# Seven-product weight chunks: where the sum of the two lower blocks is read from, and when

## The chip, the cores and the metric

The kernel runs on one core of one Trainium2 chip. The metric is device time in microseconds (us) of one execution. The kernel before took a median of 1622.32 us in 3 runs (1621.99 to 1623.5).

## The reference

One inference step of a two-layer decoder for a prompt of 512 tokens and a group of 8 single-token samples, which share all weights; the kernel treats them as 520 columns. Each layer is half a SwiGLU, a mixer, and half a SwiGLU; the first mixer pools over windows, the second is windowed attention. All data are float32. Cut to what matters here:

```
D_MODEL, D_FF, SEQ, DEC_BATCH = 1024, 2816, 512, 8

def _swiglu(x, wg, wu, wd):
    return (jax.nn.silu(x @ wg) * (x @ wu)) @ wd

for l in range(2):
    x = x + 0.5 * _swiglu(rms(x), gate[l, 0], up[l, 0], down[l, 0])
    x = x + mixer_l(rms(x))
    x = x + 0.5 * _swiglu(rms(x), gate[l, 1], up[l, 1], down[l, 1])
```

There are thus four SwiGLU blocks (called FFN 0 to 3 below), and their three weight matrices are nearly all of the bytes and of the products.

## The kernel before

**Products.** Every float32 operand is split into a high and a low part of type fp32r (`wh`, `wl` for weights; `xh`, `xl`, `th`, `tl`, `hh`, `hl`, `ph`, `pl` for activations), and a product is three matmuls: high by high, high by low, low by high. A matmul has a 128x128 weight tile and 260 columns (half of the 520). One call of `product` (line 612) takes one split weight piece of 128x512 and issues 12 matmuls.

**Seven instead of eight.** Most FFN work uses a seven-product scheme for 2x2 blocks of weights A and activations B. A hidden tile takes the gate block (upper row, A11 and A12, the two halves of the 1024 inputs) and the up block (lower row, A21 and A22); a tile of the down projection takes two blocks of 128 outputs as the two rows. The seven weight pieces are A11, A12, A22 and four sums, up to signs that lie in the activations: S1 = A21 + A22, S2 = A11 + S1, S4 = A12 + S2, S3 = A21 + A11. The 22 blocks of the hidden dimension are done in three parts of 8, 8 and 6: in each part first the hidden tiles, then (in the first two parts) four down chunks in seven products each; the third part's down projection is plain. The first 4, 3, 2 and 3 hidden tiles of FFN 0 to 3 are plain as well. That gives 76 hidden chunks and 32 down chunks in seven products, 108 in all.

**The weight pipeline** is the class `Weights` (lines 140 to 312). A *chunk* is 1 MB of weights in a tile of pool `rawp` (3 buffers of tag `raw`), loaded by DMAs that SyncE issues (`ld`, line 384): two of 512 KB for a gate/up chunk, four of 256 KB for a down chunk. A *piece* is one of the 128x512 views of a chunk; `_split` turns it into `wh` (ScalarE, line 278) and `wl` (VectorE, line 279), five pieces ahead of the product that uses it. `load(i)` issues the DMAs of chunks up to i, `add_up(i)` the sums that DMAs make. `_split` of a piece of chunk i calls `add_up` for chunk i + 1 and `load` for chunk i + 2. In `woven` (down chunks) the pieces of two neighbouring chunks interleave, and in both orders the piece A22 of a chunk is put off until A11 and S1 of the next one are out.

**The sums.** `combos` (line 194) makes them:

- S1 gets a tile `S` of its own, of 256 KB, from pool `splp` (tag `S`, 4 buffers). SyncE loads A21 into it from device memory a second time (`again`), and a DMA that GpSimd issues adds A22 to it from the chunk's `raw` tile (line 205, an accumulating DMA from SBUF to SBUF).
- S3 is made in place by another accumulating DMA on GpSimd's queue: A21 += A11 inside `raw` (line 206).
- S2 and S4 are VectorE additions in place, of A11 (line 212) and A12 (line 218). S2 reads the tile `S` and is its last reader.

Two more tiles of tag `S` hold `ph`, `pl`, activation sums of a part's first pair of hidden tiles (`HiddenSums.more`, line 655), from the second hidden tile of the part to the last product of its down projection; while they live, two `S` buffers are left for the weight chunks. The pooling mixer also borrows tiles of that tag (`pr`, `hrow`).

**Order.** The program is recorded in the order of the code; a scheduler then orders each engine's instructions, and it places each where its own estimate of time lets it. Instructions that pass through `later` keep their recorded order among each other, as do all DMAs of `ld` on SyncE's queue. Each engine's queue and SyncE's DMA queue run strictly in order: an instruction that waits holds all behind it. A tile that is taken from a pool waits for the last reader of the buffer's previous holder.

Of the kernel before, what the change touches and what calls it, by code (L numbers as in the profile page):

```python
# [11 lines left out]
F32 = mybir.dt.float32  # L12
# [3 lines left out]
ALU = mybir.AluOpType  # L16
AX = mybir.AxisListType

P = 128
# [12 lines left out]
NPL = (4, 3, 2, 3)  # L32
# [107 lines left out]
class Weights:  # L140
# [4 lines left out]
    def __init__(self, nc, rawp, splp, chunks_ahead, ahead):  # L145
        self.nc, self.rawp, self.splp = nc, rawp, splp
        self.ca, self.ahead = chunks_ahead, ahead
        self.chunks, self.items = [], []
        self.nl = self.na = self.ns = self.ng = 0
        self.late = None  # L150
        self.slow = set()
        self.part = {}
        self.stop = 10**9
        self.pin = lambda ins: ins

    def chunk(self, *dmas):
        self.chunks.append([list(dmas), None, None])
        return len(self.chunks) - 1

    def piece(self, ch, view):  # L160
# [11 lines left out]

    def load(self, i):
        while self.nl <= min(i, len(self.chunks) - 1):
            self.begin(len(self.chunks[self.nl][0]))
            self.nl += 1

    def begin(self, n):

# [14 lines left out]
    def combos(self, ch, again):  # L194

        G, V, tmp = self.nc.gpsimd, self.nc.vector, {}

        def blk(raw, r, c):
            return rows(raw)[:, r - 1, 4 * c - 4 : 4 * c, :]

        def loaded(raw):
            s1 = self.splp.tile([P, 4, P], F32, tag="S", name="S", bufs=4)
            tmp[1] = s1
            again(s1)
            G.dma_start(s1, blk(raw, 2, 2), accum_op=ALU.add)  # L205
            G.dma_start(blk(raw, 2, 1), blk(raw, 1, 1), accum_op=ALU.add)  # L206

        self.chunks[ch][2] = loaded

        def s2(raw):  # L210
            if "S2" not in tmp:
                V.tensor_tensor(blk(raw, 1, 1), blk(raw, 1, 1), tmp[1], op=ALU.add)  # L212
                tmp["S2"] = True
            return blk(raw, 1, 1)

        def s4(raw):
            s2(raw)
            V.tensor_tensor(blk(raw, 1, 2), blk(raw, 1, 2), blk(raw, 1, 1), op=ALU.add)
            return blk(raw, 1, 2)

        return {
            "A11": lambda raw: blk(raw, 1, 1),
            "S1": lambda raw: tmp[1],
            "S2": s2,
            "A12": lambda raw: blk(raw, 1, 2),
            "S4": s4,
            "S3": lambda raw: blk(raw, 2, 1),
            "A22": lambda raw: blk(raw, 2, 2),
        }
# [86 lines left out]
def yoco_step(ctx, tc, ins, outs):  # L316
    nc = tc.nc
# [3 lines left out]
    V, S, T = nc.vector, nc.scalar, nc.tensor  # L321
# [54 lines left out]
    def later(ins):  # L376

        return tc.keep_in_program_order(ins)


    W = Weights(nc, rawp, splp, 2, 5)
    W.pin_home = later

    def ld(dst, src):
        return lambda raw: later(nc.sync.dma_start(dst(raw), src))

    def plain(ch, kt, col):

        n = (kt + 1) // 2
        for k0, k1 in ((0, n), (n, kt)):  # L390
            W.piece(ch, lambda raw, k0=k0, k1=k1: raw[:, k0:k1, col : col + P])
            W.last()
# [15 lines left out]
    def plan_ffn(l, f):  # L408
        g3 = w_gate[l, f].rearrange("(k p) c -> p k c", p=P)
        u3 = w_up[l, f].rearrange("(k p) c -> p k c", p=P)  # L410
        d3 = w_down[l, f].rearrange("(k p) c -> p k c", p=P)
        t0 = 0
        for pi, n in enumerate(PARTS):
            for j in range(t0, t0 + n):
                c = slice(j * P, (j + 1) * P)
                cuts = ((0, 4), (4, 8)) if (l, f, j) == (0, 0, 0) else ((0, 8),)
                ch = W.chunk(
                    *[
                        ld(lambda raw, k=k, o=o: rows(raw)[:, o, k[0] : k[1], :], w3[:, k[0] : k[1], c])
                        for k in cuts  # L420
                        for o, w3 in ((0, g3), (1, u3))
                    ]
                )
                if j < NPL[2 * l + f]:
                    for k0 in (0, 4):
                        for o in (0, 1):
                            W.piece(ch, lambda raw, k0=k0, o=o: rows(raw)[:, o, k0 : k0 + 4, :])
                else:
                    W.sums(ch, ld(lambda t: t, u3[:, :4, c]), j == NPL[2 * l + f])
            if (2 * l + f, pi) in SEVEN:  # L430
                tiles = []
                for m in range(0, KT, 2):
                    cols = [slice((m + r) * P, (m + r + 1) * P) for r in range(2)]
                    lo, up = (slice(t0 + o, t0 + n, 2) for o in range(2))
                    ch = W.chunk(
                        *[
                            ld(lambda raw, r=r, o=o: rows(raw)[:, r, o : o + 4, :], d3[:, ks, cols[r]])
                            for o, ks in ((0, lo), (4, up))
                            for r in range(2)
                        ]  # L440
                    )
                    tiles.append((ch, W.combos(ch, ld(lambda t: t, d3[:, lo, cols[1]]))))
                W.woven(tiles)
                t0 += n
                continue
            for c in range(4):
                ch = W.chunk(ld(lambda raw, n=n: raw[:, :n, :], d3[:, t0 : t0 + n, c * 256 : (c + 1) * 256]))
                if (l, f) == (1, 1) and t0 + n == sum(PARTS) and c > 1:
                    if c == 2:
                        plain(ch, n, 0)  # L450
                    for k in range(n):
                        W.home(ch, *last_piece(k, c))
                    continue
                plain(ch, n, 0)
                plain(ch, n, P)
            t0 += n
# [4 lines left out]
    for c in range(2):  # L461
        ch = W.chunk(ld(lambda raw: raw, kv3[:, :, c * 256 : (c + 1) * 256]))
# [5 lines left out]
    for t in range(0, 8, 2):  # L468
        gp, i = t // 4, t % 4
        ch = W.chunk(  # L470
            *[
                ld(
                    lambda raw, e=e: raw.rearrange("p k (e i d) -> p k e i d", e=2, i=2)[:, :, e],
                    wq5[:, :, gp, e, i : i + 2, :],
                )
                for e in range(2)
            ]
        )
        for j in range(2):
            for k0 in (0, 4):  # L480
                W.piece(
                    ch,
                    lambda raw, j=j, k0=k0: raw.rearrange("p k (e i d) -> p k e i d", e=2, i=2)[:, k0 : k0 + 4, :, j, :],
                )
    wo5 = w_o[0].rearrange("(g e i d) c -> e d g i c", g=2, e=2, i=4)
    for g in range(2):
        for c in range(2):
            half = lambda raw: raw.rearrange("p k c -> p (k c)").rearrange("p (k c) -> p k c", k=4)
            ch = W.chunk(
                *[  # L490
                    ld(
                        lambda raw, e=e: half(raw)[e * 64 : (e + 1) * 64],
                        wo5[e, :, g, :, c * 512 : (c + 1) * 512],
                    )
                    for e in range(2)
                ]
            )
# [1578 lines left out]
```

## Time and profile before

| | |
|---|---|
| median of 3 runs | 1622.32 us |
| profiled execution: its own time | 1625.38 us |
| profiled execution: span | 1623.6 us |
| TensorE (PE) busy, share of the span | 1603.5 us, 99% |
| weight loads into TensorE (PEld) busy | 1590.5 us, 98% |
| VectorE (DVE) busy | 1415.7 us, 87% |
| ScalarE (ACT) busy | 972.4 us, 60% |
| GpSimd (POOL) busy | 258.5 us, 16% |
| granted TensorE clock, mean | 0.998 |
| read from device memory (HBM), written | 189.76 MB, 6.11 MB |

The span runs from the first to the last instruction of the profiled execution; its own time is 1.8 us longer. Matmuls overlap (one lasts 283 ns but the next one starts some 120 ns after it), so a busy PE says little by itself; where PE or PEld stands idle, time is lost. DMA queue q1 is that of the transfers that SyncE issues, q0 that of GpSimd's.

### The profile page before, as it was taken

To read this page: it belongs to the slowest core of one execution; us is meant where nothing else is said; L and a number is where in the kernel's file an instruction comes from. 1 tells how busy PE (TensorE), PEld (TensorE's weight loads), DVE (VectorE), ACT (ScalarE), POOL (GpSimd) and SP (SyncE) were. 2 spreads that over 40 slices of the span, in tenths; PEclk is the share of its full clock that TensorE was granted. 3 is DMA by queue.
4 is the path that set the end of the run, shared out by engine and by line. 5 is a ranking of instruction groups with operands and counts; after the bars stand their busy time and mean duration, and the time that the engine had idled before them with its cause. 6 is when DMAs were issued, how large, how long until landed. Compare 5 with 4: busy or idle time off the path is not lost.

```text
span 1623.6 us, 34950 instructions
## 1 busy us (share of the span) xinstructions
PE 1603.5 (99%) x13350; PEld 1590.5 (98%) x13350; DVE 1415.7 (87%) x2775; ACT 972.4 (60%) x2024; POOL 258.5 (16%) x346
## 2 busy tenths in 40 slices
PE   9999999999999999999999999999999999999997
PEld 8999999999999999999999999999999999999997
DVE  6999999879999999888899999876797989899976
ACT  6765665657665665555564565655785665565555
POOL 1111111100111111100211111100451111111100
PEclk9999999999999999999999999999999999999999
DMA  8578878753687887744878787852332577877841
GB/s 223 131 177 175 187 183 180 178 156 121 135 183 171 182 187 176 169 128 95 205 182 181 174 184 171 190 166 81 75 76 79 137 165 177 175 183 176 174 134 54
DMA packets 377364, 254.63 MB, mean 157 GB/s; under 512 B 13134, under 2 KB 343878, under 8 KB 377156
## 3 DMA queue, kind: packets, MB, share of 16 engines
q1 hardware_dynamic: 339390, 187.30, 42.1%
q0 software_dynamic: 34048, 60.00, 23.4%
q10 hardware_dynamic: 3758, 5.09, 1.0%
q8 instruction: 105, 1.72, 0.5%
q14 instruction: 63, 0.52, 0.1%
HBM read 189.76 MB, written 6.11 MB: 121 GB/s over the span
## 4 chain that ended last, share of the span: by engine, by line
PE 91%; DMA 3%; DVE 3%; ACT 1%; issue 1%; SPq 0%; POOL 0%; ACTq 0%; DVEq 0%; POOLq 0%
PE ps L619 62%; PE ps L591 23%; PE pv L1598 1%; DMA S<-raw 1%; PE pv L1173 1%; DVE wl L279 1%; DMA S<-in_ffn_w_down_dram 1%; PE pv L1218 1%; PE pv L1571 1%; PE ps L1513 1%; ACT wh L278 0%; DMA raw<-in_w_o_dram 0%; DMA xt<-in_x_prompt_dram 0%; DMA raw<-in_ffn_w_up_dram 0%; PE ps L1950 0%
## 5 line engine op out<-in xcount | busy, mean ns | idle before, releaser
L278 ACT ACTIVATE wh<-raw 128x512 fp32r<-128x512 f32 (+1 forms) x768 | 447.8, 619 | 243.8 <-DVE raw L212 68.5
L279 DVE TENSOR_TENSOR wl<-raw,wh 128x512 fp32r<-128x512 f32 (+1 forms) x768 | 500.9, 676 | 59.3 <-ACT wh L278 57.6
L619 PE MATMUL ps<-th,wh 128*128 128x260 f32 x1216 | 343.3, 283 | 1.4 <-DVE sb L780 0.5
L619 PE MATMUL ps<-tl,wh 128*128 128x260 f32 x1216 | 342.7, 283 | 0.0
L619 PE MATMUL ps<-th,wl 128*128 128x260 f32 x1216 | 341.6, 282 | 0.0
L206 POOL DMA_DIRECT2D raw<-raw x108 | 93.6, 866 | 1028.8 <-DVE wl L279 294.8
L619 PE MATMUL ps<-xh,wh 128*128 128x260 f32 x896 | 252.3, 283 | 0.9 <-ACT wh L278 0.8
L619 PE MATMUL ps<-xl,wh 128*128 128x260 f32 x896 | 251.3, 282 | 0.0
L619 PE MATMUL ps<-xh,wl 128*128 128x260 f32 x896 | 250.6, 282 | 0.0
L619 PEld LDWEIGHTS ps<-th,wh 128*128 128x128 f32 x1216 | 228.8, 188 | 2.6 <-DVE sb L780 0.7
L619 PEld LDWEIGHTS ps<-tl,wh 128*128 128x128 f32 x1216 | 228.8, 188 | 0.0
L619 PEld LDWEIGHTS ps<-th,wl 128*128 128x128 f32 x1216 | 228.2, 188 | 0.0
L619 PE MATMUL ps<-hh,wh 128*128 128x260 f32 x656 | 184.4, 284 | 2.3 <-ACT hh L370 0.9
L619 PE MATMUL ps<-hl,wh 128*128 128x260 f32 x656 | 184.3, 283 | 0.5 <-DVE hl L371 0.4
L619 PE MATMUL ps<-hh,wl 128*128 128x260 f32 x656 | 183.2, 282 | 0.0
L619 PEld LDWEIGHTS ps<-xh,wh 128*128 128x128 f32 x896 | 168.2, 188 | 2.0 <-ACT wh L278 1.6
L619 PEld LDWEIGHTS ps<-xl,wh 128*128 128x128 f32 x896 | 168.4, 188 | 0.0
L619 PEld LDWEIGHTS ps<-xh,wl 128*128 128x128 f32 x896 | 168.1, 188 | 0.0
L619 PEld LDWEIGHTS ps<-hh,wh 128*128 128x128 f32 x656 | 123.0, 188 | 3.7 <-ACT wh L278 1.2
L619 PEld LDWEIGHTS ps<-hl,wh 128*128 128x128 f32 x656 | 123.1, 188 | 1.2 <-DVE hl L371 1.1
L619 PEld LDWEIGHTS ps<-hh,wl 128*128 128x128 f32 x656 | 122.9, 188 | 0.0
L205 POOL DMA_DIRECT2D S<-raw x108 | 101.8, 942 | 116.9 <-DMA S<-in_ffn_w_down_dram 46.2
(368 smaller groups left out, 3626.8 us busy)
## 6 DMA issues: line engine op xcount, KB each, us to landing
raw<-in_ffn_w_gate_dram SPq DMA_DIRECT2D x87, 512.0 KB, 5.4
raw<-in_ffn_w_up_dram SPq DMA_DIRECT2D x87, 512.0 KB, 6.9
raw<-in_ffn_w_down_dram SPq DMA_DIRECT2D x128, 256.0 KB, 4.2
raw<-raw POOLq DMA_DIRECT2D x108, 256.0 KB, 3.6
S<-raw POOLq DMA_DIRECT2D x108, 256.0 KB, 5.1
S<-in_ffn_w_up_dram SPq DMA_DIRECT2D x76, 256.0 KB, 6.6
raw<-in_ffn_w_down_dram SPq DMA_DIRECT2D x16, 768.0 KB, 4.5
S<-in_ffn_w_down_dram SPq DMA_DIRECT2D x32, 256.0 KB, 5.7
```

The source lines that it names most:

```text
L205: G.dma_start(s1, blk(raw, 2, 2), accum_op=ALU.add)
L206: G.dma_start(blk(raw, 2, 1), blk(raw, 1, 1), accum_op=ALU.add)
L278: pin(nc.scalar.activation(dh, src, AF.Copy))
L279: pin(nc.vector.tensor_tensor(dl, src, dh.bitcast(F32), op=ALU.subtract))
L591: ins = T.matmul(banks[:, hf, :H], a[:, kk, :], hcols(b, hf), start=(first and i == 0), stop=(last and i == 2),)
L619: T.matmul(bank[:, :H], a[:, kk, :], b, start=(not more and kk == 0 and i == 0), stop=(kk == 3 and i == 2), skip_group_check=more,)
L1173: later(T.matmul(o, a[:, c], b[:, kk, :], start=(n == 0), stop=(n == 5)))
L1218: later(T.matmul(o, zz[tau][z][:, c], b, start=(i == 0), stop=(i == len(lst) - 1)))
L1513: later(T.matmul(o, q_[rows, qc], k_[rows, kc_], start=(i == 0), stop=(i == 2)))
L1571: later(T.transpose(self.both[bi][:, kt * 256 + e * P : kt * 256 + (e + 1) * P], z, ident))
L1598: later(T.matmul(o, a, p_[:, kc_], start=(n == 0), stop=(n == 3 * len(kts) - 1)))
```

## The change

The sum S1 is made wholly out of device memory, and its two transfers are issued ahead of the chunk's own. `combos` no longer gets one function for A21 but two (`sum_of`): SyncE loads A21 into the tile `S`, and GpSimd's accumulating DMA adds A22 from device memory, not from the `raw` tile. They move out of `add_up`'s function `loaded` into a new one, `prepared`, that `load` calls through `prepare` just ahead of the chunk's own DMAs. The tile `S` is taken there too, so its buffer belongs to the chunk from that point on. The sum S3 stays in `loaded`. The counts of instructions and of transfers on each engine stay the same; what is read from device memory grows by 108 times 256 KB.

```
+    def prepare(self, i):
+        while self.np <= min(i, len(self.chunks) - 1):
+            if self.chunks[self.np][3]:
+                self.chunks[self.np][3]()
+            self.np += 1
...
     def load(self, i):
         while self.nl <= min(i, len(self.chunks) - 1):
+            self.prepare(self.nl)
             self.begin(len(self.chunks[self.nl][0]))
             self.nl += 1
...
+        def prepared():
+            tmp[1] = self.splp.tile([P, 4, P], F32, tag="S", name="S", bufs=4)
+            again[0](tmp[1])
+            again[1](tmp[1])
+
         def loaded(raw):
-            s1 = self.splp.tile([P, 4, P], F32, tag="S", name="S", bufs=4)
-            tmp[1] = s1
-            again(s1)
-            G.dma_start(s1, blk(raw, 2, 2), accum_op=ALU.add)
             G.dma_start(blk(raw, 2, 1), blk(raw, 1, 1), accum_op=ALU.add)

         self.chunks[ch][2] = loaded
+        self.chunks[ch][3] = prepared
...
+    def sum_of(a, b):
+
+        return [ld(lambda t: t, a), lambda t: nc.gpsimd.dma_start(t, b, accum_op=ALU.add)]
...
-                    W.sums(ch, ld(lambda t: t, u3[:, :4, c]), j == NPL[2 * l + f])
+                    W.sums(ch, sum_of(u3[:, :4, c], u3[:, 4:, c]), j == NPL[2 * l + f])
...
-                    tiles.append((ch, W.combos(ch, ld(lambda t: t, d3[:, lo, cols[1]]))))
+                    tiles.append((ch, W.combos(ch, sum_of(d3[:, lo, cols[1]], d3[:, up, cols[1]]))))
```

The instructions of PE and of VectorE stand in the same order in both programs. On ScalarE one load of the pooling mixer's data stands seven instructions earlier. SyncE and GpSimd change throughout. First SyncE's queue before, at the first down projection of FFN 1 (the numbers behind a tile's name are those of the program; raw41 is the part's last gate/up chunk, raw42 to raw44 are its first down chunks):

```order
L385 DMA raw41_6345<-in_ffn_w_gate_dram 128x8x128
L385 DMA raw41_6345<-in_ffn_w_up_dram 128x8x128
L385 DMA S_6426<-in_ffn_w_up_dram 128x4x128
L385 DMA raw42_6486<-in_ffn_w_down_dram 128x4x128 x4
L385 DMA S_6569<-in_ffn_w_down_dram 128x4x128
L385 DMA raw43_6638<-in_ffn_w_down_dram 128x4x128 x4
L385 DMA S_6721<-in_ffn_w_down_dram 128x4x128
L385 DMA raw44_6782<-in_ffn_w_down_dram 128x4x128 x4
```

and the same place now (raw43_6641 and S_6638 are the chunk that had raw43_6638 and S_6721):

```order
L394 DMA S_6345<-in_ffn_w_up_dram 128x4x128
L394 DMA raw41_6348<-in_ffn_w_gate_dram 128x8x128
L394 DMA raw41_6348<-in_ffn_w_up_dram 128x8x128
L394 DMA S_6486<-in_ffn_w_down_dram 128x4x128
L394 DMA raw42_6489<-in_ffn_w_down_dram 128x4x128 x4
L394 DMA S_6638<-in_ffn_w_down_dram 128x4x128
L394 DMA raw43_6641<-in_ffn_w_down_dram 128x4x128 x4
L394 DMA S_6782<-in_ffn_w_down_dram 128x4x128
```

Each load of S has moved from behind its chunk's own loads to ahead of them. GpSimd's queue before, for the same chunks:

```order
L206 DMA raw42_6486<-raw42_6486 128x512
L205 DMA S_6569<-raw42_6486 128x512
L206 DMA raw43_6638<-raw43_6638 128x512
L205 DMA S_6721<-raw43_6638 128x512
L206 DMA raw44_6782<-raw44_6782 128x512
L205 DMA S_6951<-raw44_6782 128x512
```

and now:

```order
L398 DMA S_6486<-in_ffn_w_down_dram 128x4x128
L214 DMA raw42_6489<-raw42_6489 128x512
L398 DMA S_6638<-in_ffn_w_down_dram 128x4x128
L214 DMA raw43_6641<-raw43_6641 128x512
L398 DMA S_6782<-in_ffn_w_down_dram 128x4x128
L214 DMA raw44_6785<-raw44_6785 128x512
```

The addition to S has moved ahead of the chunk's other sum, reads device memory in place of `raw`, and depends on nothing of the chunk's own loads. In the part 0 of FFN 0, where the first three seven-product chunks raw4 to raw6 are loaded, SyncE's queue was

```order
L385 DMA S_540<-in_ffn_w_up_dram 128x4x128
L385 DMA raw5_544<-in_ffn_w_gate_dram 128x8x128
L385 DMA raw5_544<-in_ffn_w_up_dram 128x8x128
L385 DMA S_723<-in_ffn_w_up_dram 128x4x128
L385 DMA raw6_727<-in_ffn_w_gate_dram 128x8x128
L385 DMA raw6_727<-in_ffn_w_up_dram 128x8x128
L385 DMA S_962<-in_ffn_w_up_dram 128x4x128
```

and is

```order
L394 DMA S_359<-in_ffn_w_up_dram 128x4x128
L394 DMA raw4_362<-in_ffn_w_gate_dram 128x8x128
L394 DMA raw4_362<-in_ffn_w_up_dram 128x8x128
L394 DMA S_544<-in_ffn_w_up_dram 128x4x128
L394 DMA raw5_547<-in_ffn_w_gate_dram 128x8x128
L394 DMA raw5_547<-in_ffn_w_up_dram 128x8x128
L394 DMA S_727<-in_ffn_w_up_dram 128x4x128
L394 DMA raw6_730<-in_ffn_w_gate_dram 128x8x128
```

Here S_727, which takes the buffer of S_359, now stands ahead of the loads of its own raw6.

More of the change, by code (lines that the diff above doesn't have):

```diff
@@ L148, in __init__ @@
         self.chunks, self.items = [], []
-        self.nl = self.na = self.ns = self.ng = 0
+        self.nl = self.na = self.ns = self.ng = self.np = 0
         self.late = None
@@ L156, in chunk @@
     def chunk(self, *dmas):
-        self.chunks.append([list(dmas), None, None])
+        self.chunks.append([list(dmas), None, None, None])
         return len(self.chunks) - 1
```

## Prediction

> **What bounds the kernel now.** First the page's first part, then the DMA queues of its third part:
>
> ```profile
> span 1623.6 us, 34950 instructions
> PE 1603.5 (99%) x13350; PEld 1590.5 (98%) x13350; DVE 1415.7 (87%) x2775; ACT 972.4 (60%) x2024; POOL 258.5 (16%) x346
> q1 hardware_dynamic: 339390, 187.30, 42.1%
> q0 software_dynamic: 34048, 60.00, 23.4%
> ```
>
> TensorE is the bound: PEld stands idle for 33 us of the span, and no faster transfer can give more than that. The change touches only the seven-product stretches, so I cut the span into the four that lie between the mixers, FFN 0 to 3 without their ends:
>
> ```profile
> core 0: us, PE busy (x) PEld busy (x) DVE busy (x) ACT busy (x) POOL busy (x), PEclk, DMA share, GB/s
> 43.00:330.00 287.00, 286.24 (x2375) 285.04 (x2374) 264.54 (x488) 171.71 (x345) 45.05 (x54) 1.00 0.77 175
> 407.00:700.00 293.00, 291.26 (x2416) 289.81 (x2415) 269.42 (x504) 173.95 (x351) 46.27 (x54) 1.00 0.77 169
> ...
> sum 1160.00, PE 1153.70 PEld 1148.62 DVE 1061.70 ACT 686.00 POOL 181.65; mean PE 288.42 PEld 287.15 DVE 265.42 ACT 171.50 POOL 45.41
> ```
>
> PEld is idle there for 1160 - 1148.62 = 11.4 us: the ceiling of any gain here. VectorE is 92% busy (1061.70 of 1160), so a late split is caught up with slowly; the transfers fill 0.77 of the 16 DMA engines.
>
> Is S1 late at all? The waits of ScalarE say yes, and the chain of waits shows what that does at one place, the down projection of FFN 1's part 0:
>
> ```profile
> ACT wh L278 <- DMA S<-raw: 38.5, 22, 3.7
> 465.14 0.61 DVE raw L212
> 467.29 6.58 DMA S<-in_ffn_w_down_dram
> 474.49 4.54 DMA S<-raw
> 479.14 0.64 ACT wh L278
> 488.03 7.04 PE ps L619 x55
> ```
>
> In 22 places ScalarE, ready to split S1, waits for the sum, 38.5 us in all. Splitting runs five pieces ahead, so most of this never reaches PE. At 467.29 the load of S goes out behind its chunk's four loads and takes 6.58 us, the addition 4.54 us; ScalarE, an in-order queue, starts at 479.14, and everything behind it (splits, copies out of PSUM) is late until PE is level again at 488.03. I then read the waits in a window round each place where PEld waits shortly after a late S1. Six have them (222-232, 474-490, 600-609, 993-999, 1492-1498 and 1545-1558, in this order):
>
> ```profile
> PEld ps L619 <- DVE hl L371: 0.4, 1, 0.4
> PEld ps L619 <- ACT sa L799: 0.3, 1, 0.3
> ...
> ACT wh L278 <- DMA S<-raw: 3.5, 1, 3.5
> PEld ps L619 <- ACT hh L370: 1.1, 1, 1.1
> PEld ps L619 <- DVE hl L371: 0.4, 1, 0.4
> PEld ps L619 <- ACT xh L370: 0.3, 1, 0.3
> ...
> PEld ps L619 <- DVE hl L371: 0.3, 1, 0.3
> ...
> PEld ps L619 <- ACT sa L807: 0.4, 1, 0.4
> ...
> PEld ps L619 <- ACT sa L807: 1.3, 1, 1.3
> ...
> PEld ps L619 <- DVE sb L780: 0.7, 1, 0.7
> PEld ps L619 <- ACT sa L770: 0.7, 1, 0.7
> ```
>
> In sum 0.7 + 1.8 + 0.3 + 0.4 + 1.3 + 1.4 = 5.9 us. The waits name ScalarE and VectorE, not a DMA: these are the instructions queued behind the late split. The other 5.5 us of the 11.4 follow no late S1, and I leave them as they are.
>
> **The change, part by part.** *S1 earlier.* Nothing of S1 waits for `raw` any more. Its load can go out as soon as the chunk before it has been issued and the buffer is free, that is after the line 212 addition of the chunk that held it. Where `ph` and `pl` live, that is two chunks back. At the place above and at 1470-1482 the queues read:
>
> ```profile
> 464.45 0.69 DVE L279 TENSOR_TENSOR wl<-raw,wh 128x512 fp32r<-128x512 f32 x1
> 465.05 0.69 DVE L212 TENSOR_TENSOR raw<-raw,S 128x512 f32<-128x512 f32 x1
> 465.17 2.02 SPq L385 DMA_DIRECT2D raw<-in_ffn_w_down_dram  x4
> 470.15 0.86 POOL L206 DMA_DIRECT2D raw<-raw  x1 [2.87 <-DVE raw L218]
> 474.98 0.63 ACT L278 ACTIVATE wh<-raw 128x512 fp32r<-128x512 f32 x1
> 1472.34 0.69 DVE L212 TENSOR_TENSOR raw<-raw,S 128x512 f32<-128x512 f32 x1
> 1481.76 0.95 SPq L385 DMA_DIRECT2D S<-in_ffn_w_down_dram  x1
> 1488.51 7.08 DMA S<-raw
> ```
>
> At 465 the buffer is free at 465.74, so S goes out 1.5 us earlier and no longer behind four loads. With the median landings of the page's DMA issues,
>
> ```profile
> raw<-in_ffn_w_down_dram SPq DMA_DIRECT2D x128, 256.0 KB, 4.2
> S<-raw POOLq DMA_DIRECT2D x108, 256.0 KB, 5.1
> ```
>
> 4.2 us for a 256 KB load, 0.6 us until GpSimd issues (473.87 to 474.49 above) and 5.1 us for an addition, S1 is there at 465.8 + 9.9 = 475.7 instead of 479.03: 3.3 of ScalarE's 3.5 us. I count two thirds of the 1.8 us, and of the 0.7 and 0.3 us at the two places of the same kind (second down chunk of a part, at 222 and 600): 1.9 of 2.8 us. At 1472 the chunk is the fourth of the down projection; its buffer is free at 1473.0, 8.7 us ahead of the present issue, and S1 would be there near 1483, against 1495.59 (1488.51 + 7.08). The place at 993 is the fourth down chunk too. At 1545 the buffer is that of part 1's `ph`, free long before. Those three go wholly: 0.4 + 1.3 + 1.4 = 3.1 us. Gain: 5.0 us.
>
> *The chunk's own loads later.* They now stand behind S and its wait. At 465.17 `raw` goes out when `wl` of 464.45 ends; the addition behind it ends 0.6 us later, and issuing S takes some 0.5 us: 1.1 us late. Cover: the split of `raw`'s own pieces; ScalarE takes this chunk's first one at 474.98, right after GpSimd had all its loads at 470.15, and 4.8 us hide 1.1. The longest hold is in FFN 0, where the third S takes the first one's buffer:
>
> ```profile
> 47.46 0.37 SPq L385 DMA_DIRECT2D raw<-in_ffn_w_gate_dram  x1
> 59.41 0.37 SPq L385 DMA_DIRECT2D S<-in_ffn_w_up_dram  x1
> 56.79 1.23 POOL L206 DMA_DIRECT2D raw<-raw  x1
> 76.07 0.66 ACT L278 ACTIVATE wh<-S 128x512 fp32r<-128x512 f32 x1
> ```
>
> The loads of 47.46 wait until about 59.4, 12 us; with 9.3 us from issue to GpSimd's use of them (47.46 to 56.79) they are there at 69, and the first piece is split just ahead of S1, which stands at 76.07: 6 us of cover left. SyncE's queue holds nothing else in that time. I take 0 for both; the upper bound is under the slower rivals.
>
> *The addition out of device memory.* Before: 128 packets of 2 KB; now 512 of 512 B, the length of a run of columns in device memory. From the queue rows q0 spends at most 0.234 x 16 x 1623.6 / 216 = 28.1 us of DMA engine on an addition (178 ns a packet), and a packet of q1, nearly all of them 512 B, takes 0.421 x 16 x 1623.6 us / 339390 = 32.2 ns. No row has an addition in 512 B packets. Low end: same bytes, same time, 28.1 us. High end: each packet still takes 178 ns, 91.4 us. I take the low end: the 2 KB additions cost 28.1 / (512 x 0.0322) = 1.7 times plain packets of the same bytes, and 512 x 32.2 ns x 1.7 = 28.0 us. So the DMA share stays at 0.77, and device memory gives 108 x 256 KB = 28 MB more to 189.76 MB read. GpSimd's issue:
>
> ```profile
> L205 POOL DMA_DIRECT2D S<-raw x108: 855/872/1237, 35.0 to 1549.7; - x108
> ```
>
> 872 ns with 128 rows; with four times as many, between 0.9 and 3.5 us, and POOL, 45 us busy of 290 a stretch, takes 26 x 2.6 us more at worst. At 3.5 us S1 at 465 would be there 2.6 us later, 0.7 us ahead of before: that is the bound at which the 1.9 us shrink to little. *Moved on ScalarE:* one load of the pooling mixer, 0.3 us of sequencer, at 0.
>
> The sum, against the profiled span: 1623.6 - 5.0 = 1618.6. The profiled execution's own time, 1625.38, stands 3.1 above the median, so I apply the difference to the median: 1622.3 - 5.0 = 1617.3 us. Late next, where S1 no longer is: VectorE's bursts at the start of each down projection.
>
> **The rivals.** *Hidden anyway.* The six waits are VectorE's bursts, which S1 only happens to precede; at 92% busy they come a little later all the same. Only the three places where S1 is early by 8 us gain, and half of it: 1.5 us, 1620.8. For it: no wait of PEld names a DMA. Against: at 479.14 ScalarE sits idle 3.5 us for S1 alone.
>
> *By the skill's rule on GpSimd's descriptors.* GpSimd writes them through a port that VectorE can hold, and four times as many would be exposed to it; if a 3.5 us issue came out at each addition, only the 3.1 us stay: 1619.2. Against it: 108 issues beside a 92% busy VectorE lie within 855 to 1237 ns. The Trainium skill, SBUF — State Buffer, "Who interferes with whom", says that copies and casts in VectorE's two-port modes block GpSimd for the whole instruction, tensor_tensor not its writes; the trace, where nearly all of VectorE is TENSOR_TENSOR, agrees by that narrow spread.
>
> *Slower, the additions fill the DMA engines.* At 178 ns a packet, each addition takes 63.3 us more; 26 in a stretch are 63.3 x 26 / (16 x 290) = 0.35 of its time, 0.77 + 0.35 = 1.12, and each stretch would grow by at least 0.12 x 290 = 35 us: near 1760. It decides from where the room of 0.23 is used up: 0.23 x 16 x 290 / 26 = 41 us an addition, 135 ns a packet.
>
> *Slower, the chunk's loads.* Behind S's wait they become the late ones, and it decides from a delay above the 4.8 us of cover. If loads at 0.77 share land that late, the eight down projections and the hidden chunks pay for their 1.1 us: 8 x 1.1 for the down projections less the 3.1 us gain = +5.7, 1628. Against it stand the two covers above.
>
> **How the numbers follow.** 0.2% (3.2 us) is about what a measurement of this kernel can tell from no change. Forecast: 0.54. Hidden anyway 0.20 and the descriptor rule 0.05, both within 0.2% (1619.2 counted there). The additions 0.08, the loads 0.13: slower. So faster 0.54, same 0.25, slower 0.21. The likeliest case's own range is 1611 (all 11.4 us of idle PEld gone) to 1620; the range reaches to 1625 over the two cases of no change and leaves out most of the slower ones.
>
> **What would show it.** Right: the addition's row reads device memory, ScalarE's waits for S fall from 38.5 us to under 10, PEld's waits at the six places from 5.9 to about 1, and q0 holds 108 x (512 - 128) = 41,472 more packets at an unchanged share. Wrong: q0's share well above 23%; ScalarE waiting for `raw` at the first piece of a chunk; SyncE waiting for line 212's addition with `raw` loads landing after their split was due.

## The result, and the profile after

The changed kernel takes 1618.44 us (median of 10 runs, 1617.69 to 1620.21) against 1622.91 us before, measured beside it: a ratio of 0.9971, 95% interval 0.9964 to 0.9979, that is 4.7 us less (3.4 to 5.8). The forecast was 1617.3 us and 5.0 us less. The profiled execution took 1619.61 us, against 1625.38 us for the profile before; these two stand 5.8 us apart, somewhat more than the medians, and the profile before is slower than each of the ten timed runs of that kernel (at most 1624.92 us).

The first and third parts of its page, the four stretches of the seven products (one row of four, and their sum), and the rows of ScalarE's list of waits that name a transfer of weights:

```profile
span 1617.8 us, 35069 instructions
PE 1602.7 (99%) x13350; PEld 1591.9 (98%) x13350; DVE 1415.0 (87%) x2775; ACT 974.7 (60%) x2024; POOL 308.1 (19%) x346
q1 hardware_dynamic: 339390, 187.30, 41.8%
q0 software_dynamic: 75520, 60.00, 25.8%
```

```profile
43.00:330.00 287.00, 286.56 (x2385) 285.89 (x2385) 265.38 (x489) 172.12 (x345) 54.70 (x52) 1.00 0.79 174
...
sum 1160.00, PE 1157.22 PEld 1154.30 DVE 1062.72 ACT 687.49 POOL 222.38; mean PE 289.31 PEld 288.57 DVE 265.68 ACT 171.87 POOL 55.59
```

```profile
ACT wh L287 <- DMA raw<-in_ffn_w_down_dram: 6.1, 4, 2.8
...
ACT wh L287 <- DMA S<-in_ffn_w_down_dram: 0.7, 1, 0.7
```

(Line 287 is the old line 278, 632 the old 619.) In the stretches PEld is idle for 1160 - 1154.30 = 5.7 us, half of the 11.4 before. ScalarE's 38.5 us of waits for S1 are down to 0.7 in this list. Two more, of 1.0 and 1.2 us, are listed under VectorE though S1 landed 0.1 us before they ended, so that some 2.8 us are left, in three places, all at the second down chunk of a part:

```profile
222.94 0.63 ACT L287 ACTIVATE wh<-S 128x512 fp32r<-128x512 f32 x1 [0.96 <-DVE g L787]
1343.62 0.64 ACT L287 ACTIVATE wh<-S 128x512 fp32r<-128x512 f32 x1 [1.19 <-DVE g L787]
```

What is new is that it waits 6.1 us, in 4 places, for the chunk's own loads.

In the six windows of the prediction, moved by the time that the program is ahead there, PEld's list of waits has one row left, at the place near 474:

```profile
PEld ps L632 <- ACT hh L379: 0.7, 1, 0.7
```

So 5.9 us have become 0.7. A finer measure is possible because TensorE's 13350 matmuls stand in the same order in both programs: the start of each can be compared between the two traces. The changed program gains 1.1 us near 227, 1.2 near 485, 0.6 near 605, 0.4 near 995, 1.3 near 1495 and 1.5 near 1552, nothing worth naming elsewhere in the stretches, and loses 1.3 us in the attention mixer, which the change doesn't touch; a second profile of the changed kernel (below) has not that loss.

The queues at two of the places, SyncE, GpSimd and ScalarE:

```profile
464.46 0.37 SPq L394 DMA_DIRECT2D S<-in_ffn_w_down_dram  x1
464.93 2.20 SPq L394 DMA_DIRECT2D raw<-in_ffn_w_down_dram  x4
468.46 1.30 POOL L398 DMA_DIRECT2D S<-in_ffn_w_down_dram  x1 [8.01 <-DVE hl L380]
475.19 0.63 ACT L287 ACTIVATE wh<-S 128x512 fp32r<-128x512 f32 x1 [0.91 <-PE ps L632]
1470.34 0.37 SPq L394 DMA_DIRECT2D S<-in_ffn_w_down_dram  x1
1475.34 1.30 POOL L398 DMA_DIRECT2D S<-in_ffn_w_down_dram  x1 [2.81 <-DVE wl L288]
1476.91 2.35 SPq L394 DMA_DIRECT2D raw<-in_ffn_w_down_dram  x4
```

At 464.46 S goes out, 4.0 us later GpSimd issues the addition, and its landing at 473.44 (the trace's end of that transfer) is 1.7 us ahead of ScalarE's split, which now waits for a product of TensorE. At 1470.34 the load of S leaves 6.6 us ahead of the chunk's own loads, which still wait for their buffer.

### The profile page after: what moved, and what is told of

Its sections match the earlier page's. It is cut to its first block, busy times and chain, and to the rows that moved or that the text cites. A ratio compares the mean times of both kernels' runs of the same rounds, so it can differ in the third digit from the quotient of the medians.

```text
span 1617.8 us, 35069 instructions
## 1 busy us (share of the span) xinstructions
PE 1602.7 (99%) x13350; PEld 1591.9 (98%) x13350; DVE 1415.0 (87%) x2775; ACT 974.7 (60%) x2024; POOL 308.1 (19%) x346
## 3 DMA queue, kind: packets, MB, share of 16 engines
q0 software_dynamic: 75520, 60.00, 25.8%
## 4 chain that ended last, share of the span: by engine, by line
PE 98%; ACT 1%; DVE 1%; DMA 0%; issue 0%; POOL 0%; SPq 0%; DVEq 0%; ACTq 0%; POOLq 0%
PE ps L632 67%; PE ps L604 23%; PE pv L1611 1%; PE pv L1186 1%; PE pv L1584 1%; PE pv L1231 1%; PE ps L1526 1%; PE ps L1963 0%; PE ps L1970 0%; DMA raw<-in_ffn_w_gate_dram 0%; PE ps L560 0%; ACT wh L287 0%; PE pv L1717 0%; PE ps L1067 0%; PE ps L1873 0%
## 5 line engine op out<-in xcount | busy, mean ns | idle before, releaser
L398 POOL DMA_DIRECT2D S<-in_ffn_w_up_dram x76 | 101.2, 1331 | 465.5 <-DMA S<-in_ffn_w_up_dram 143.0
```

The lines of the kernel that those rows point to most:

```text
L398: return [ld(lambda t: t, a), lambda t: nc.gpsimd.dma_start(t, b, accum_op=ALU.add)]
```

## The experiments

Theory A says that S1's arrival at the six places is the gain. Rival B says that it is spread over all 108 chunks. Rival C says that the source is what matters: an addition that waits for none of its chunk's loads. In all kernels here TensorE and VectorE run their instructions in the same order as before.

### Which chunks

`six` gives the new S1 to the six chunks of the six places alone; `rest`, with `not in`, to the other 102:

```
+SIX = (17, 32, 44, 74, 101, 106)
...
+        early = n in SIX
...
         def loaded(raw):
+            if not early:
+                tmp[1] = self.splp.tile([P, 4, P], F32, tag="S", name="S", bufs=4)
+                again[0](tmp[1])
+                G.dma_start(tmp[1], blk(raw, 2, 2), accum_op=ALU.add)
             G.dma_start(blk(raw, 2, 1), blk(raw, 1, 1), accum_op=ALU.add)
...
+        if early:
+            self.chunks[ch][3] = prepared
```

> Only the six chunks whose late S1 stands ahead of the six places of the prediction (numbers 17, 32, 44, 74, 101 and 106 of the 108) get S1 out of device memory and ahead of their own loads; the other 102 are as in the kernel before. Theory A (the gain is S1's arrival at those six places): nearly the whole gain of the changed kernel, 3.5 to 5 us less than before, ratio 0.997 to 0.998, and ScalarE still waits for S some 20 us elsewhere without PE losing anything by it. Rival B (the gain is spread over all chunks: the shorter way of all sums): 6 of 108 parts of it, under 0.5 us, ratio 0.9995 to 1.000.

> The complement: 102 chunks as in the changed kernel, the six as before. Theory A: none of the gain, 0 to 1 us less than before, ratio 0.9995 to 1.0005, with PEld's waits at the six places still 5 to 6 us. Rival B: nearly the whole gain, ratio 0.997 to 0.9975. If some other chunk's load, now ahead, crowds the six, slower than before by up to 1 us.

Measured: `six` 0.9987 (0.9978 to 0.9996), 2.1 us less; `rest` 0.9980 (0.9971 to 0.9989), 3.2 us less. Neither theory holds as it was put: the two parts share the gain, and together give about the whole (0.0033 against 0.0029).

The profile of `six` does show the full gain at all six places, 6.1 us by the starts of the matmuls, and loses 0.6 us each at three others, near 318, 685 and 976. The profile of `rest`, the slowest of its eleven runs, gains at four of the six places without a change of their chunks (0.5 us near 227, 1.1 near 485, 1.3 near 1495, 1.5 near 1552), and loses 1.6 us at a fifth, near 995, where its S1 comes later than before. ScalarE's waits for S1 in these two, of 38.5 us before:

```profile
ACT wh L300 <- DMA S<-raw: 15.5, 10, 2.6
```

```profile
ACT wh L300 <- DMA S<-raw: 9.3, 4, 3.2
```

In `rest` the untouched chunk 101 has its addition in 5.4 us from issue to landing, against 7.1 before, and chunk 106 in 4.8 against 9.4, but chunk 74 in 8.1 against 6.5. So S1 can come earlier or later at a chunk that was not changed. What Theory A had wrong is that only a chunk's own change moves its S1; that the time lost goes with S1's arrival holds, as the next section shows.

### Do the places stay?

`before2` is a second profile of the kernel before, `eight` gives the new S1 to the second down chunk of each part alone, `eight2` is a second profile of it, `after2` one of the changed kernel.

```
+EIGHT = (5, 17, 32, 44, 60, 72, 87, 99)
...
+        early = n in EIGHT
```

> The kernel before, a second profile. If the six places are fixed by the program, PEld's waits there come again, 5 to 7 us in sum, and ScalarE's waits for S are again about 38 us in some 22 places. If they hang on how the transfers happen to meet, some of the six are gone and others have come.

> Only the second down chunk of each part (numbers 5, 17, 32, 44, 60, 72, 87, 99 of the 108) gets S1 out of device memory and ahead of its own loads. From the profiles so far a wait of ScalarE for S there costs PE about 0.2 us up to a wait of 2.5 us, 0.7 us at 3, 1.8 us at 3.7 and 4.8 us at 6. Theory A3 (by this curve): the waits there fall from some 2.2 to under 1 us, which gives the 2.5 us that they cost in the two profiles of before, and the places at 1492 and 1545 stay: 1.5 to 3 us less than before, ratio 0.998 to 0.999. Rival B (spread over all): 8 of 108 parts, 0.3 us, ratio 0.9998.

> The kernel with the eight second down chunks changed, a second profile. Its first profile shows nearly the gain of the whole change at the six places (4.7 us against the first profile of before), though its median gained 1.5 us. If the rest is lost at places that change from one execution to the next, the second down chunks are again on time here, and PE loses 0.5 us or more at two or more places that the first profile of this kernel does not show, each behind a late S1 of one of the 100 other chunks. If the six places hold in every execution, both profiles show the same stalls and the same time within 0.5 us.

> The changed kernel, a second profile. If the profile on which the reading rests is typical, ScalarE's waits for S are again under 10 us in sum, none over 1.5 us, and the gain against the first profile of before comes again at the same places: near 227, 483, 604, 995, 1495 and 1550 us.

`before2` took 1623.91 us. PEld's waits in the six windows (222-232, 474-490, 600-609, none in 993-999, 1492-1498, 1545-1558):

```profile
PEld ps L619 <- DVE hl L371: 0.2, 1, 0.2
PEld ps L619 <- ACT hh L370: 0.9, 1, 0.9
PEld ps L619 <- DVE hl L371: 0.4, 1, 0.4
PEld ps L619 <- DVE hl L371: 0.3, 1, 0.3
...
PEld ps L619 <- ACT sa L807: 0.7, 1, 0.7
PEld ps L619 <- ACT sa L770: 0.8, 1, 0.8
PEld ps L619 <- DVE sb L780: 0.7, 1, 0.7
```

4.0 us in place of 5.9: one of the six is gone, three are smaller, and there is a new loss near 318. `eight` is 0.9989 (0.9979 to 0.9998), 1.8 us less, inside what A3 expected; the 0.9998 of B is the end of the interval. Its profile, though, shows 4.7 us less than the first profile of before, and the place at 1545, which A3 expected to stay, gains its 1.5 us in both profiles of this kernel, with chunk 106 untouched. `eight2` took 1622.56 us, 1.6 us more than the execution in the profile of `eight`. The second down chunks are on time again, but by the matmuls' starts it loses 1.1 us near 658 and 0.7 us near 995, where the first profile does not, and each time an S1 of the untouched kind has come late (chunks 49 and 74):

```profile
658.74 0.63 ACT L300 ACTIVATE wh<-S 128x512 fp32r<-128x512 f32 x1 [2.68 <-PE ps L645]
995.52 0.63 ACT L300 ACTIVATE wh<-S 128x512 fp32r<-128x512 f32 x1 [1.17 <-DMA S<-raw]
```

(At 658.74 the profile names a product of TensorE, but the addition landed at 658.64, 0.1 us before this split, the same distance as where the profile does name S.)

Place by place the time follows S1. In each cell stands ScalarE's idle time just before the split of S1, then what TensorE gains at that place against the first profile of before (by the matmuls' starts), in us; the columns are the chunks of the six places:

| profile | 17 | 32 | 44 | 74 | 101 | 106 |
|---|---|---|---|---|---|---|
| `before` | 3.7, - | 3.5, - | 3.2, - | 0.9, - | 1.9, - | 3.4, - |
| `before2` | 3.0, 0.7 | 3.0, 0.6 | 3.1, 0.1 | 0.0, 0.4 | 1.2, 0.6 | 3.5, -0.2 |
| `rest` | 3.2, 0.5 | 2.5, 1.1 | 3.1, 0.1 | 2.5, -1.6 | 0.4, 1.3 | 0.1, 1.5 |
| `eight` | 1.2, 1.1 | 0.9, 1.2 | 0.8, 0.5 | 0.0, 0.4 | 1.5, 0.3 | 0.1, 1.5 |
| `eight2` | 0.7, 1.1 | 0.9, 1.2 | 0.8, 0.5 | 1.2, -0.3 | 1.3, 0.5 | 0.1, 1.5 |
| `after` | 1.0, 1.1 | 0.9, 1.2 | 0.7, 0.6 | 0.0, 0.4 | 0.0, 1.3 | 0.1, 1.5 |

The less ScalarE waits for S1 at a place, changed chunk or not, the more of the gain is there; where it waits longer than before (chunk 74 in `rest` and `eight2`), time is lost. Why an untouched S1 moves can be read at chunk 106, first in `before`, then in `eight`:

```profile
1539.08 0.37 SPq L385 DMA_DIRECT2D raw<-in_ffn_w_gate_dram  x1
1539.32 0.98 POOL L205 DMA_DIRECT2D S<-raw  x1
```

```profile
1534.78 0.93 POOL L225 DMA_DIRECT2D S<-raw  x1
1535.89 0.37 SPq L407 DMA_DIRECT2D raw<-in_ffn_w_gate_dram  x1
```

In the first, SyncE issues the next chunk's loads 0.2 us ahead of the addition, which takes 9.4 us; in the second 1.1 us behind it, and it takes 5.4. Chunk 49 does the same (5.7 us in `eight`, 8.4 in `eight2`, with the loads 1.9 us behind and 0.2 us ahead), chunk 101 in `rest` does not. Over 13 profiles (all here but `halves`, below) an addition out of `raw` takes 6.7 us by the median where a chunk's load goes out from 1.5 us ahead of it to 0.5 us behind it, 5.0 where one goes out 0.5 to 2 us behind it and none nearer, and 3.9 otherwise. No run sets this order on purpose, so it is read off, not tested.

So part of the loss is at fixed places and part moves from one execution to the next. The spread of the runs fits: 23 runs of before lie within 6.2 us, 12 of `eight` within 6.2, 11 of `six` and of `rest` within 3.8 and 5.0, and 10 of the changed kernel within 2.5 us. In `after2` (1618.70 us) the list has 1.8 us of ScalarE's waits for S1, and the gains stand at the same six places. In both profiles of the changed kernel the 100 S1 that are not of a second down chunk land 4.7 us or more before their split; that this is why the moving part is gone is argued from the traces.

### One half of the change at a time

`source` reads A22 from device memory but leaves both transfers where they were, behind the chunk's loads; `order` moves the load of S ahead but adds from the `raw` tile; `behind` is the changed kernel with the load of S put back behind its chunk's loads. The lines of code show each against the changed kernel.

```
 source:
-        def prepared():
+        def loaded(raw):
             tmp[1] = self.splp.tile([P, 4, P], F32, tag="S", name="S", bufs=4)
             again[0](tmp[1])
             again[1](tmp[1])
-
-        def loaded(raw):
             G.dma_start(blk(raw, 2, 1), blk(raw, 1, 1), accum_op=ALU.add)
...
-        self.chunks[ch][3] = prepared
 order:
         def prepared():
             tmp[1] = self.splp.tile([P, 4, P], F32, tag="S", name="S", bufs=4)
             again[0](tmp[1])
-            again[1](tmp[1])
...
         def loaded(raw):
+            G.dma_start(tmp[1], blk(raw, 2, 2), accum_op=ALU.add)
             G.dma_start(blk(raw, 2, 1), blk(raw, 1, 1), accum_op=ALU.add)
 behind:
+            self.begin(len(self.chunks[self.nl][0]))
             self.prepare(self.nl)
-            self.begin(len(self.chunks[self.nl][0]))
```

> Only the source is changed: the addition to S reads A22 out of device memory in 512-byte packets, but load and addition are issued where the kernel before issues them, behind the chunk's own loads. Theory A: S1 comes when it came before or some 0.8 us later (0.43 us more for GpSimd's issue, 5.6 us of DMA engine more over 16 engines), so no gain: -0.3 to +1 us, ratio 0.9998 to 1.0007. Rival C (what matters is that the addition no longer waits for the chunk's loads and no longer reads the tile that the other sum is reading): most of the gain, ratio 0.997 to 0.998.

> Only the order is changed: the tile S is taken and A21 loaded ahead of the chunk's own loads, but the addition reads A22 from the raw tile, so it waits for the chunk's loads. Theory A: at the three second down chunks the addition can follow the other sum at once (471.0 in place of 474.49 at the place near 474), so these give most of their 2.8 us; at the three other places it follows the chunk's loads, 1.6 us earlier than before or less, so about half of 3.1 us: in sum 3 to 4 us less than before, ratio 0.9975 to 0.998. Rival C: nothing, 0.9995 to 1.0005.

> The changed kernel with one thing put back: SyncE issues the load of S behind its chunk's own loads, as before; the addition still reads device memory and stands ahead of nothing of its chunk on GpSimd's queue, as before. Theory A2 (S1 is due early only at the second down chunk of each part, and there the load of S behind four loads plus an addition that takes a microsecond longer comes too late): as the run in which only the source changed, 15 to 30 us more than before, ratio 1.010 to 1.018. Rival D (that run lost its time because its addition held the chunk's other sum on GpSimd's queue, which here goes first): -2 to +3 us, 0.9988 to 1.002.

Measured: `source` 1.0159 (1.0145 to 1.0172), 26 us more than before. `order` 1.0088 (1.0074 to 1.0102), 14 us more. `behind` 1.0171 (1.0152 to 1.0190), 28 us more. Theory A had the first two wrong by 25 and 17 us, rival C fell altogether, and A2 had `behind` right. Two changes that each cost more than ten microseconds gain 4.7 together.

`behind` does not test rival D, though. In the traces of `source` as of `behind` GpSimd issues the chunk's other sum ahead of the addition to S at all 108 chunks, as in the kernel before; what D held against `source` did not happen there, and that is why D falls. SyncE's and ScalarE's instructions stand in the same order in the two but for one load of S, so that `behind` is nearly a repetition of `source`. In the changed kernel the addition goes first at all 108, in `order` at the 76 hidden chunks alone. What this third part of the change is worth by itself no run shows.

The queue rows show where the time goes. `source`, then `behind`, then `order`, each at a second down chunk:

```profile
470.46 0.75 SPq L391 DMA_DIRECT2D S<-in_ffn_w_down_dram  x1
478.39 1.30 POOL L395 DMA_DIRECT2D S<-in_ffn_w_down_dram  x1 [4.04 <-DVE wl L285]
485.65 0.63 ACT L284 ACTIVATE wh<-S 128x512 fp32r<-128x512 f32 x1 [6.89 <-DMA S<-in_ffn_w_down_dram]
```

```profile
475.89 0.93 SPq L394 DMA_DIRECT2D S<-in_ffn_w_down_dram  x1
483.95 1.30 POOL L398 DMA_DIRECT2D S<-in_ffn_w_down_dram  x1 [4.02 <-DVE wl L288]
490.32 0.63 ACT L287 ACTIVATE wh<-S 128x512 fp32r<-128x512 f32 x1 [5.64 <-DMA S<-in_ffn_w_down_dram]
```

```profile
592.03 0.69 DVE L221 TENSOR_TENSOR raw<-raw,S 128x512 f32<-128x512 f32 x1
593.12 0.37 SPq L394 DMA_DIRECT2D S<-in_ffn_w_down_dram  x1
593.62 3.42 SPq L394 DMA_DIRECT2D raw<-in_ffn_w_down_dram  x4
602.08 0.86 POOL L213 DMA_DIRECT2D S<-raw  x1 [0.88 <-DMA raw<-in_ffn_w_down_dram]
607.23 0.63 ACT L287 ACTIVATE wh<-S 128x512 fp32r<-128x512 f32 x1 [6.02 <-DMA S<-raw]
```

In `source` and `behind` the load of S still stands behind four loads (7.9 and 8.1 us from issue to GpSimd's addition, 7.2 before), and the addition takes 7.2 and 6.3 us to land, against 4.5 before. ScalarE's wait near 480 is 6.9 and 5.6 us, where it was 3.5. In `order` the chunk's loads stand behind S's wait for its buffer (VectorE's addition of line 221, to 592.72), and the addition stands behind those loads: it is issued 9.0 us after the load of S, against 4.0 in the changed kernel. The medians over the eight second down chunks say the same:

| | load of S to GpSimd's issue, us | addition, us | load of S to S1, us |
|---|---|---|---|
| `before` | 5.9 | 3.5 | 9.8 |
| `source` | 7.1 | 4.5 | 12.3 |
| `behind` | 7.5 | 5.4 | 12.8 |
| `order` | 8.9 | 4.5 | 13.3 |
| `after` | 3.8 | 5.2 | 9.0 |

The addition out of device memory is slower in the changed kernel too; what S1 gains there is the shorter way to GpSimd's issue and the earlier start. Set against the matmul that TensorE has reached, the load of S goes out 1.2 to 2.7 us earlier than before, in `order` as in the changed kernel, and the chunk's own loads 0.6 to 2.0 us later. Moved ahead, S makes the chunk's loads late; only an addition that needs none of them doesn't pay for it.

How can a few microseconds of waiting cost 14 to 28 us here and so little before? For each pair of neighbouring matmuls I took the smallest distance of their starts over the same 13 profiles as undisturbed, and summed what lies above it (over 0.03 us) from 3 us before to 16 us after the split of S1, at the eight second down chunks of each profile:

| ScalarE's idle time before that split, us | places | mean loss of TensorE, us |
|---|---|---|
| 0 to 1.2 | 54 | 0.1 |
| 1.2 to 2.5 | 17 | 0.2 |
| 2.5 to 3.3 | 13 | 0.7 |
| 3.3 to 4.2 | 7 | 1.8 |
| 4.2 to 5.5 | 6 | 2.7 |
| over 5.5 | 7 | 4.8 |

Up to some 2.5 us the pieces that are split ahead hide the wait; beyond that each microsecond costs about one. The kernel before stood at the bend: its longest waits there were 3.0 to 3.7 us. The same sum over a whole profile is 10.0 and 8.6 us for the two of before, 4.3 and 3.3 for the two of after, 20.1 for `order`, 31.6 for `source` and 39.7 for `behind`, in step with the measured times. Of these, the eight second down chunks alone hold 4.1 and 2.5, 0.9 and 0.9, 16.1, 21.4 and 27.1 us: most of what the three kernels lose is lost there.

### A microsecond more, at eight chunks or at a hundred

`hold_second` delays S1 in the changed kernel by a copy on GpSimd at the eight second down chunks, `hold_others` (`not in`) at the other 100.

```
+SECOND = (5, 17, 32, 44, 60, 72, 87, 99)
...
+        held = n in SECOND
...
             again[0](tmp[1])
+            if held:
+                G.tensor_copy(tmp[1][:, :2], tmp[1][:, :2])
             again[1](tmp[1])
```

> The changed kernel, and at the second down chunk of each part (8 of 108 chunks) GpSimd copies half of the tile S onto itself between the load and the addition, which makes S1 about 1 us later there and moves nothing else. Theory A2: these eight S1 have under 2 us to spare, so 2 to 6 us more than the changed kernel, ratio to before 0.9985 to 1.001. Rival B (no chunk matters more than another): nothing that shows, ratio 0.997 to 0.9975.

> The same copy at the 100 other chunks and not at the eight. Theory A2: these S1 have 5 to 25 us to spare in the changed kernel's trace, so a microsecond costs nothing: as the changed kernel, ratio to before 0.9965 to 0.998. Rival B: each pays its part, and 100 of them pay more than 3 us, ratio 0.999 or above; so would a copy that takes VectorE's port.

Measured: `hold_second` 0.9973 (0.9964 to 0.9983), `hold_others` 0.9980 (0.9971 to 0.9988). The first lies with its whole interval below what A2 expected (0.9985 and above), and where B had it; the second lies at the end of what A2 expected, and with its whole interval below what B did (0.999 and above). So neither theory has both runs right, and neither run is clearly apart from the changed kernel's 0.9971. The rows say what they were worth: ScalarE's waits in `hold_second`, and the copies and the stretches in `hold_others`.

```profile
ACT wh L297 <- DMA S<-in_ffn_w_down_dram: 8.0, 5, 3.3
```

```profile
L220 POOL COPY S<-S 128x256 f32<-128x256 f32 x100 | 106.0, 1060 | 557.2 <-DMA S<-in_ffn_w_up_dram 326.2 <-DMA S<-in_ffn_w_down_dram 58.9 <-DVE wl L298 38.9
sum 1160.00, PE 1157.10 PEld 1153.84 DVE 1072.22 ACT 687.51 POOL 317.25; mean PE 289.27 PEld 288.46 DVE 268.06 ACT 171.88 POOL 79.31
```

The waits of `hold_second` reach 3.3 us once, where the curve has at most 0.7 us: a delay within the reserve is not felt. `hold_others` added something else than a delay: VectorE is busy 9.5 us longer (1072.22 against 1062.72) beside GpSimd's copies. It is the copies: the 286 VectorE instructions that overlap one last 12.0 us longer in sum than in the changed kernel's profile, all the others together 0.04 us.

### Smaller packets

`halves` cuts each addition of the changed kernel into two of 128 columns' halves:

```
+        def add(t):
+            o, i = (z.rearrange("p k (h c) -> p k h c", h=2) for z in (t, b))
+            for h in range(2):
+                nc.gpsimd.dma_start(o[:, :, h], i[:, :, h], accum_op=ALU.add)
+
+        return [ld(lambda t: t, a), add]
```

> The changed kernel with each addition cut into two of 512 packets of 256 bytes, one for each half of the columns. GpSimd issues 1.3 us more for each. If a packet costs its time and not its bytes (66 ns each), q0 takes 34 us of DMA engine more for each chunk, the DMA share in the stretches goes from 0.78 to about 0.9, and S1 comes 3 us later: at the second down chunks waits of about 4 us, 8 times 2 us more, 10 to 20 us more than the changed kernel (ratio to before 1.003 to 1.010). If packets cost by their bytes, S1 comes 1.3 us later and the curve gives 1 to 3 us more than the changed kernel (0.998 to 0.999). Rival (the engines fill up): over 30 us more, above 1.015, with the chunks' own loads late.

Measured: 0.9976 (0.9967 to 0.9985), not clearly apart from the changed kernel; the case of 0.998 to 0.999 isn't excluded. q0, the first stretch, and ScalarE's wait for S1:

```profile
q0 software_dynamic: 132544, 60.01, 31.3%
43.00:330.00 287.00, 286.55 (x2386) 285.89 (x2385) 265.84 (x490) 172.85 (x347) 87.07 (x77) 1.00 0.87 175
ACT wh L287 <- DMA S<-in_ffn_w_down_dram: 1.2, 2, 0.7
```

The DMA share rises to 0.84 to 0.87 in the four stretches, and TensorE loses nothing by it. The expected delay of S1 of 1.3 to 3 us did not come: from the load of S to S1 it takes 10.2 us by the median of all 108 chunks, against 9.7 in the changed kernel, and 9.0 in both at the second down chunks. At each chunk the second half is issued before the first has landed, so the two are under way side by side. The rival of filled engines finds no support up to this share; where it would begin was not tried.

## Why the prediction came out right, step by step

**The ceiling and the six places.** Half of the 11.4 us of idle PEld came back, and the waits at the six places fell from 5.9 to 0.7 us, where the prediction had "about 1" and a gain of 5.0. The mechanism was right: place by place the gain goes with S1's arrival. What the step lacked is that a place in one profile is not a place in every execution: the second profile of before has 4.0 us there and loses elsewhere, and the six chunks alone gave 2.1 us by medians (`six`). The 5.0 us were added up from one execution, slower than each of the ten runs that stand beside the result. That 4.7 came so near is therefore in part luck: the six chunks alone gave less, and the losses that move, which the prediction did not count, made up for it.

**S1's new time.** At the place near 465 it was put at 465.8 + 9.9 = 475.7. It is 464.46 + 9.0 = 473.44 in a program that is 1.3 us ahead: the load took 4.0 us to GpSimd's issue (4.8 forecast), the addition 5.0 (5.1 forecast), so S1 is 1.0 us better than forecast. At 1473 the forecast was a load at 1473.0 and S1 near 1483; with the program 2.5 us ahead they are 1470.34 and 1479.96. Right.

**The two-thirds.** Of the 2.8 us at the three second down chunks I counted 1.9 for S1. All of it came, 2.8 us by the starts of the matmuls. The curve says why the fraction was too small: the waits there, 3.2 to 3.7 us, all stood above the bend.

**The chunk's loads at 0.** The delay itself was forecast rightly: at 465 the chunk's loads go out 1.1 us later against TensorE's progress. The 0 is right in the sum, thinner than I said, and one of the prediction's own signs of being wrong did show: ScalarE waits 6.1 us in 4 places for them, at most 2.8 us, where the cover of 4.8 us was to hide all. At that longest place PEld waits no longer than before:

```profile
PEld ps L632 <- ACT wh L287: 1.1, 2, 0.9
```

in the window 1462-1482, against 1.2 us in the profile of before. q0 has 75520 - 34048 = 41472 packets more, as forecast. The longest hold came as forecast too, with the loads at 59.63 (59.4 forecast). So what comes next is not only VectorE's bursts, as I wrote, but these loads.

**The addition.** I took the low end, 28.1 us of DMA engine. From the two q0 rows it takes (0.258 x 1617.8 - 0.234 x 1623.6) x 16 / 108 = 5.6 us more, 33.7 us or 66 ns a packet: mis-sized by a fifth, and q0's share, which was to stay unchanged, rose from 23.4% to 25.8%. The 178 ns a packet of the high end was itself misread: it is the mean of all 34048 packets of q0, of which some 6400 belong to no addition. By the trace's packet records the 2 KB packets took 211 ns before, so the high end would have been 108 us and not 91.4; the 33.7 measured are far from either. GpSimd's issue is 1.3 us:

```profile
L398 POOL DMA_DIRECT2D S<-in_ffn_w_down_dram x32: 1293/1302/1321, 84.3 to 1475.3; - x32
```

Ahead of the chunk's loads this cost nothing that shows, as forecast. Harmless in itself, as the sum took it to be, it is not: `source` pays 26 us.

**The rivals.** *Hidden anyway* fell: all six places gained, in both profiles of the changed kernel. *The skill's rule on descriptors* did not come true: the issues lie within 1293 and 1321 ns at the down projections (1293 to 1653 at the others), beside a 92% busy VectorE. The rule on which it rested, the Trainium skill, SBUF — State Buffer, "Who interferes with whom", leaves GpSimd's writing of descriptors free beside tensor_tensor (which the page calls inferred), and the trace agrees. *The additions fill the DMA engines* fell: a share of 0.78, and up to 0.87 in `halves` at no cost that shows. *The chunk's loads* as the loser came true in `order`, where the addition depends on them, and not in the changed kernel.

## What to carry to other kernels

Ask of a transfer moved to the head of a queue what it pushes back, and who needs that: here the early load delays its chunk's own loads, which is free only because the same edit made the sum independent of them. Each half alone cost 14 to 28 us. A wait that is shorter than the reserve of work prepared ahead (here some 2.5 us) costs nothing, and beyond it nearly all of it, so read a profile's waits against the reserve. Before a loss is priced by place, take a second profile: part of it moves between executions, here, as far as the traces tell, with the order in which two queues happen to issue.

## What the runs showed of the hardware that was not expected

- An accumulating packet of 512 bytes out of device memory takes 66 ns of a DMA engine, one of 256 bytes 46 ns ((0.313 x 1617.6 - 0.258 x 1617.8) x 16 / 108 = 13.2 us more for twice the packets, 46.9 us for 1024); the trace's packet records give 66 and 46 ns too. Half the bytes take 0.7 of the time. The Trainium skill, DMA: Bandwidth & Descriptors, "Why small descriptors are slow (HBM only)", has three cycles of overhead for each packet beside one for 32 bytes, which by an estimate would be 11 to 19 cycles, 0.58; for these accumulating packets the measured share of a fixed part is larger.
- The addition out of device memory too depends on when SyncE's loads go out: 7.2 us by the median of 222 with a chunk's load issued from 1.5 us ahead of it to 0.5 us behind it, 6.2 with one 0.5 to 2 us behind it, 5.0 otherwise.
- An addition cut into two transfers comes at most 0.5 us later by the median, although it takes 13.2 us more of the 16 engines' time together.
- GpSimd's 100 copies of 128x256, 1.06 us each, make VectorE 9.5 us longer busy, about 0.1 us a copy. The Trainium skill, SBUF — State Buffer, "Who interferes with whom", says that a VectorE instruction with two inputs in SBUF contends with a GpSimd instruction that reads SBUF; these copies, beside tensor_tensor, agree with it.
